# Other queues and moments for layer 0's loads of tables, u and bias, a corner set once, and a priority for evacuations: a two-layer encoder trunk on one core

## The chip, the core and the metric

The kernel runs on one core of a Trainium2 chip. The metric is device time in microseconds of one execution of the whole program. A core has a TensorE (PE) for matmuls and transposes, a VectorE (DVE), a ScalarE (ACT), a GpSimd (POOL), and a SyncE (SP) that only issues DMAs. Each of them works through its own list of instructions in a fixed order, and an instruction that waits holds up everything behind it in that list. DMAs are issued from a list too: here from SP's, and some from POOL's.

## The reference

Two layers work on a sequence of 256 frames of width 2048, in float32. Layer 0 makes one projection of the normalised input, cut into q, k, v for an attention of 16 heads x 64, u for a state-space branch (S5), and two gates:

```
proj = rmsnorm(x) @ w_in                 # q | k | v | u | z_A | z_B
s    = q k^T / sqrt(64) + bias           # own chunk of 64 frames and the chunks before it
o_a  = softmax(s) v * silu(z_A)
x_t  = Abar x_{t-1} + Bbar u_t           # complex, 64 groups of 16 channels, one state of 64 each
y    = gelu(Re(C x_t) + D u_t)
o_b  = y * sigmoid(y @ w_glu + b_glu) * silu(z_B)
x    = x + concat(o_a, o_b) @ w_out
```

With 256 frames every frame sees its own chunk of 64 and all earlier ones, so the score block of frames 0 to 63 against frames 64 to 127 is masked. Layer 1 is an attention with forget gates (16 heads x 128), with its own input projection, gate and output projection. A last RMSNorm follows.

## The kernel before

**Weights.** All weights stream through the core once, in tiles of 128 x 1024 float32 (512 KB), one such tile to a *chunk*. `next_w` (line 148) loads a tile from SP's queue into one of four buffers, and a split makes of it a high half (`wh`, ACT, line 164) and a low half (`wl`, DVE, line 165), three buffers each. The split is given priority over other work (`SPLIT_AHEAD`, 3000). `project` (line 168) runs a projection over 16 or 8 blocks of 128 rows, two blocks to a chunk, with three matmuls for each block and each half of the tokens (lines 175 to 177): twelve matmuls of 128 x 512 in a chunk. A projection has two accumulators in PSUM, out of three; after its last chunk the function `evac` empties them (line 191).

**The task clock.** PE's order is written by hand. `tick()` (line 141) counts chunks. Other work is put into tasks, generators that run at a given chunk and say with `yield n` that they go on n chunks later; `at_chunk(c, task)` files one. What a task issues for PE stands at this place between the chunks. For the other engines and for the DMA queues a planner sets the order, from its own estimate of times and from priorities. `high_priority(offset)` raises the priority of an instruction, and `keep_in_program_order` pins a DMA in its queue at its place in the program's order. The chunks of layer 0: u 0 to 15, the first gate `za` 16 to 23, q 24 to 31, k, v, then za, q, k, v of the second half of the heads at 48 to 79, the gate `zb` 80 to 95, the attention's output projection `oa` from 96.

**S5.** `setup_task` (line 724) computes small tables and loads the first two `bc` (B and C of eight groups, 256 KB). `tables(e, ...)` (line 343), for e from 0 to 7, works a `bc` into larger tables on DVE and ACT (lines 351 to 380), stores `mx` to DRAM (`m_d`, line 381), and after `gap` chunks (12 for the first, 6 for the others) transposes on PE (`pm`), a product `pk`, four stores of `ks` to DRAM (`k_d`, line 402), the next `tables`, and the load of `bc` e + 2 (line 408). There are two buffers of `bc`. After a further wait (`READY`: the first one not before chunk 28) come `pv`, transposes, and copies to the state `X`. `u_in` (line 434) starts at chunk 16. It loads u back from DRAM as `un` (four loads on SP's queue, line 439), spreads it on ACT seven chunks later (`spread`, line 443, behind the newest split in ACT's order), and transposes it two chunks on (`pu`, line 456; the last two of four a chunk after the first two) into `uT`. From chunk 64 `load_T` and `load_mo` (lines 632 and 639) read the stored tables back from POOL's queue.

**Attention of layer 0.** The 16 heads are worked in two halves (`a0`, `a1`), each in four pairs of heads. `pair(hp)` (line 579) loads the bias tile `bt` (128 x 2 x 256, two buffers, each load into a fresh tile, line 584), sets its masked corner of 64 partitions x 64 columns on POOL (line 585), turns q and k two chunks later (`pqk`), makes the scores a chunk after that (`psc`), lets `probs` (line 523) do the softmax on DVE and ACT, and turns the result four chunks later (`turn_probs`, `pp`, line 547). `mix` (line 601) multiplies by v. The list at line 752 says at which chunk each pair and mix starts. `gate_T` (line 494) is the first gate: evacuated by ACT with SiLU (line 500), then turned (`pz`). `load_xa` (line 711) brings the residual input into the buffers that q, k, v and a gate leave.

**Layer 1** (from line 820) runs four groups of four heads, each with projections q, k, v and z of 16 blocks.

Of the kernel before, what the change touches and what calls it, by code (L numbers as in the profile page):

```python
# [9 lines left out]
F32 = mybir.dt.float32  # L10
# [7 lines left out]
P = 128  # L18
L = 256
# [4 lines left out]
NEG = -1.0e30  # L24
# [14 lines left out]
SPLIT_AHEAD = 3000  # L39
# [4 lines left out]
def trunk(ctx: ExitStack, tc: tile.TileContext, a, out: bass.AP):  # L44
    nc = tc.nc
# [73 lines left out]
    def at_chunk(c, task):  # L119

        seq[0] += 1
        queue.append((c, seq[0], task))
        if not busy:
            run_due()
# [16 lines left out]
    def tick():  # L141
        clock[0] += 1
        run_due()
# [4 lines left out]
    def next_w(split=None, dst=None):  # L148
        i = wpos[0]
        wpos[0] += 1  # L150
        raw = wp.tile([P, CK * NT], F32, name=f"wr_{i}", tag="wr", bufs=4)
        if dst:
            wh, wl = dst
        else:
            wh = wp.tile([P, CK * NT], F32R, name=f"wh_{i}", tag="wh", bufs=3)
            wl = wp.tile([P, CK * NT], F32R, name=f"wl_{i}", tag="wl", bufs=3)
        step = NT if split else CK * NT
        for o in range(0, CK * NT, step):
            c = slice(o, o + step)
            nc.sync.dma_start(raw[:, c], a["w"][i][:, c])  # L160
            if split:
                split(o // NT)
            with tc.high_priority(offset=SPLIT_AHEAD):
                last_split[:] = [nc.scalar.activation(wh[:, c], raw[:, c], AF.Copy)]  # L164
                nc.vector.tensor_tensor(wl[:, c], raw[:, c], wh[:, c].bitcast(F32), op=ALU.subtract)  # L165
        return wh, wl

    def project(ah, al, nkb, name, evac, ready=None, by_token=False):

        acc = [ps_acc.tile([P, NT], F32, name=f"acc_{name}_{t}", tag="acc") for t in range(2)]  # L170

        def block(kb, wh, wl, t):
            c = slice(kb % CK * NT, (kb % CK + 1) * NT)
            sh, sl = ah[:, kb, t * P:(t + 1) * P], al[:, kb, t * P:(t + 1) * P]
            nc.tensor.matmul(acc[t], sh, wh[:, c], start=kb == 0, stop=False)  # L175
            nc.tensor.matmul(acc[t], sh, wl[:, c], start=False, stop=False)  # L176
            nc.tensor.matmul(acc[t], sl, wh[:, c], start=False, stop=kb == nkb - 1)  # L177

        if by_token:
            for t in range(2):  # L180
                for kb in range(nkb):
                    block(kb, *ready[kb // CK], t)
            return acc
        for kc in range(nkb // CK):
            wh, wl = ready[kc] if ready else next_w()
            kbs = range(kc * CK, (kc + 1) * CK)
            for kb, t in [(kb, t) for kb in kbs for t in range(2)] if ready else [(kb, t) for t in range(2) for kb in kbs]:
                block(kb, wh, wl, t)
            if kc == nkb // CK - 1:
                for t in range(2):  # L190
                    evac(t, acc[t])
            tick()


# [4 lines left out]
    at = l0.enter_context(tc.tile_pool(name="at", bufs=2))  # L199
# [137 lines left out]

    def load_bc(e):
        bc = s5.tile([P, 8, 4, GC], F32, name=f"bc_{e}", tag="bc", bufs=2)
        tc.keep_in_program_order(nc.sync.dma_start(bc, a["s5bc"][:, e * 8:e * 8 + 8]))  # L340
        return bc

    def tables(e, bc, gap, ready):
# [35 lines left out]
        V.tensor_tensor(tm, pw(pi, fwd), wide(bc[:, :, 3, :], 8), op=ALU.mult)  # L379
        V.tensor_tensor(mx[:, :, 1:9, :], mx[:, :, 1:9, :], tm, op=ALU.add)  # L380
        nc.sync.dma_start(m_d[e], mx[:, :, 1:9, :].rearrange("p s l c -> p s (l c)"))

        yield gap

# [18 lines left out]
        if e == 7:  # L403
            at_chunk(clock[0], s5_tail())
        else:
            at_chunk(clock[0], tables(e + 1, bcs[e + 1], GAPS[e + 1], READY[e + 1]))
            if e < 6:
                bcs.append(load_bc(e + 2))
        yield max(2, ready - clock[0])

        pv = ps_s.tile([P, 2, P], F32, name=f"pv_{e}", tag="s")
# [15 lines left out]
            nc.scalar.copy(X[:, 1:, w, e * 8:e * 8 + 8],  # L427
                           pt[:, w].rearrange("p k (g n) -> p n (k g)", n=NCH))

    GAPS, READY = (12, 6, 6, 6, 6, 6, 6, 6), (28, 0, 0, 0, 0, 0, 0, 0)  # L430
    uT = s5b.tile([P, NGQ, P], F32, name="uT")
    un = X = None

    def u_in():

        nonlocal un, X
        un = res.tile([P, TC, G * GC // 4], F32, name="un", tag="X")
        for g4 in range(4):
            nc.sync.dma_start(un[32 * g4:32 * g4 + 32],
                              u_d[:, g4 * 256:(g4 + 1) * 256].rearrange("(n j) f -> n j f", j=TC))  # L440
        un4s = []

        def spread(b):
            un4 = s5b.tile([P, 4, TC, GC], F32, name=f"un4_{b}", tag="vs", bufs=2)
            with tc.issue_after(last_split[0].ins):
                nc.scalar.copy(un4, un[:, ::-1, b * 64:(b + 1) * 64].rearrange("p j (k c) -> p k j c", c=GC))
            un4s.append(un4)

        yield 7
        spread(0)  # L450
        spread(1)
        yield 2
        for b in range(4):
            pu = ps_s.tile([P, 4, P], F32, name=f"pu_{b}", tag="s")
            for k in range(4):
                nc.tensor.transpose(pu[:, k, :], un4s[b][:, k].rearrange("p j c -> p (j c)"), ident)
            nc.scalar.copy(uT[:, b * 4:b * 4 + 4, :], pu)
            if b < 2:
                spread(b + 2)
            if b == 1:  # L460
                yield 1
        X = res.tile([P, NCH + 1, 2, G], F32, name="X", tag="X")
        nc.gpsimd.memset(X[:, 0], 0.0)
# [50 lines left out]
    def scores(qT, kT, rows, keys):  # L514

        pscs = [ps_s.tile([P, 3, P], F32, name=f"psc_{key}", tag="s") for key in keys]
        for psc, r in zip(pscs, rows):
            nc.tensor.matmul(psc[:, 0, :], qT[r, 0:P], kT[r, 0:P], start=True, stop=True)
        for psc, r in zip(pscs, rows):
            nc.tensor.matmul(psc[:, 1:3, :], qT[r, P:L], kT[r, 0:L], start=True, stop=True)  # L520
        return pscs
# [41 lines left out]
            nc.vector.tensor_tensor(dl[:, kb + k, :], po[:, k], dh[:, kb + k, :].bitcast(F32), op=ALU.subtract)  # L563

    rbx = a["rbx"]

    class Half:

# [10 lines left out]
        def pair(self, hp):  # L579

            hf = self.hf
            h0 = hf * 8 + hp * 2
            bt = at.tile([P, 2, L], F32, name=f"bt_{hf}_{hp}", tag="bt")
            nc.sync.dma_start(bt, bass.AP(rbx.tensor, rbx.offset + h0 * 384, [[1, P], [384, 2], [1, L]]))
            nc.gpsimd.memset(bt[0:64, :, 0:64], NEG)
            yield 2
            pqk = ps_s.tile([P, 2, L], F32, name=f"pqk_{hf}_{hp}", tag="s")
            for w, src in ((0, self.q), (1, self.k)):
                for t in range(2):
                    nc.tensor.transpose(pqk[:, w, t * P:(t + 1) * P], src[:, t, hp * P:(hp + 1) * P], ident)  # L590
            qkT = at.tile([P, 2, L], F32, name=f"qkT_{hf}_{hp}", tag="qkT")
            nc.scalar.copy(qkT, pqk)
            yield 1
            pscs = scores(qkT[:, 0, :], qkT[:, 1, :], [slice(0, 64), slice(64, 128)], [f"a{h0}", f"a{h0 + 1}"])
            lgs = [probs(at, pscs[hh], bt[:, hh, P - 1::-1], bt[:, hh, ::-1], f"a{h0 + hh}", scaled=True)
                   for hh in range(2)]
            yield 4
            for hh in range(2):
                self.work.append(turn_probs(at, lgs[hh], f"a{h0 + hh}", scaled=True))
# [27 lines left out]
    a0, a1 = Half(0), Half(1)  # L627
# [83 lines left out]
    def load_xa(n):  # L711
        t_ = at.tile([P, 2, NT], F32, name=f"xa_{n}", tag=("qk", "qk", "v", "za")[n], bufs=(2, 2, 1, 3)[n])
        nc.sync.dma_start(t_, xin[:, :, n * NT:(n + 1) * NT])
        xa.append(t_)

    def load_xas(*ns):
        for n in ns:
            load_xa(n)
        yield None
# [11 lines left out]
    bcs = []  # L731
# [18 lines left out]
    at_chunk(clock[0], u_in())  # L750

    for c, task in ((39, a0.pair(0)), (43, a0.pair(1)), (49, a0.mixes(0)), (47, a0.pair(2)), (52, a0.mixes(1)),
                    (51, a0.pair(3)), (56, a0.mixes(2)), (60, a0.mixes(3)),
                    (71, a1.pair(0)), (75, a1.pair(1)), (81, a1.mixes(0)), (79, a1.pair(2)), (84, a1.mixes(1)),
                    (83, a1.pair(3)), (88, a1.mixes(2)), (92, a1.mixes(3)), (93, load_xas(0, 1, 2)), (96, load_xas(3))):
        at_chunk(c, task)
    zb = []
    a0.zaT = gate_T(0)
# [26 lines left out]
    for n in range(2):  # L785
# [4 lines left out]
        def evac(t, acc):  # L790
            V.tensor_tensor(ob[:, t, :], acc, bg, op=ALU.add)
            nc.scalar.activation(ob[:, t, :], ob[:, t, :], AF.Sigmoid)
            V.tensor_tensor(ob[:, t, :], ob[:, t, :], zb[n][:, t, :], op=ALU.mult)
# [223 lines left out]
    acc = project(oTh, oTl, 16, "oo3", None, held, by_token=True)  # L1017
# [95 lines left out]
```

## Time and profile before

| | us |
|---|---|
| median of three runs | 968.06 (966.23 to 968.22) |
| the profiled execution, its own time | 967.27 |
| its span, first to last instruction | 965.6 |
| TensorE busy | 933.5 |
| VectorE busy | 579.4 |
| ScalarE busy | 517.0 |
| GpSimd busy | 104.4 |

The profile is one execution. Its page lists busy times and the costliest groups of instructions; other views of the same trace list who waited for whom, the instructions of an engine in order of time, and the busy time of every engine in a stretch. A wait is noted with the instruction that waited, what released it, the total, the number of times and the longest one. In the timelines the columns are start, duration, engine, line, operation, output from inputs, the count of merged instructions, and in brackets the idle time before with what ended it. In the table of stretches the columns are the stretch, its length, the busy time (and instructions) of PE, PE's weight loads, DVE, ACT and POOL, then the granted clock of TensorE as a share of full speed, the busy share of the DMA engines, and GB/s.

### The profile page before, as it was taken

How to read it: one execution, taken by the hardware profiler on the slowest of the kernel's cores; microseconds unless marked ns; L12 is line 12 of the kernel's file. 1: busy time of each engine (PE TensorE's matmuls, PEld its weight loads, DVE VectorE, ACT ScalarE, POOL GpSimd, SP SyncE). 2: the span in 40 equal slices, each digit the busy share in tenths (PEclk: the TensorE clock that was granted, in tenths of full speed). 3: DMA queues.
4: the chain of work that ended last, by engine and by line, in shares of the span. 5: the costliest groups of instructions: out<-in, count | busy, mean ns of one | idle time of the engine just before them, and what ended most of it. 6: DMA issues, size and time to landing. Idle time of an engine off the chain costs nothing.

```text
span 965.6 us, 13241 instructions
## 1 busy us (share of the span) xinstructions
PE 933.5 (97%) x4814; PEld 758.8 (79%) x4814; DVE 579.4 (60%) x1023; ACT 517.0 (54%) x817; POOL 104.4 (11%) x177
## 2 busy tenths in 40 slices
PE   6997999999998999999999999999999999999995
PEld 5885777777776678788888888888888888888884
DVE  7886678755798346665755545454545454545573
ACT  6636556864464666455645644464446444644451
POOL 2000000000652000200001400040004000200210
PEclk9999999999999899999999999999999999999998
DMA  9877566645999468655556555555554556455552
GB/s 326 289 222 230 178 203 203 193 156 185 227 232 305 161 224 247 219 174 182 179 195 226 174 186 174 190 171 186 173 193 148 184 173 194 152 182 171 195 197 88
DMA packets 68546, 190.43 MB, mean 197 GB/s; under 512 B 7936, under 2 KB 22512, under 8 KB 68096
## 3 DMA queue, kind: packets, MB, share of 16 engines
q1 hardware_dynamic: 65056, 181.07, 58.4%
q0 software_dynamic: 3424, 8.51, 3.5%
q8 instruction: 38, 0.62, 0.3%
q14 instruction: 28, 0.23, 0.1%
HBM read 180.09 MB, written 9.45 MB: 196 GB/s over the span
## 4 chain that ended last, share of the span: by engine, by line
PE 85%; DVE 4%; DMA 3%; ACT 3%; issue 3%; SPq 1%; POOL 0%; POOLq 0%; DVEq 0%; ACTq 0%
PE acc_cq L175 3%; PE acc_cv L177 3%; PE acc_ck L175 3%; PE acc_cq L177 3%; PE acc_cv L176 3%; PE acc_cz L177 3%; PE acc_cv L175 3%; PE acc_cq L176 3%; PE acc_cz L175 3%; PE acc_ck L177 3%; PE acc_ck L176 3%; PE acc_cz L176 3%; PE acc_oo L177 3%; PE acc_oo L175 3%; PE acc_oo L176 3%
## 5 line engine op out<-in xcount | busy, mean ns | idle before, releaser
L165 DVE TENSOR_TENSOR wl<-wr,wh 128x1024 fp32r<-128x1024 f32 (+1 forms) x292 | 361.4, 1238 | 288.1 <-ACT wh L164 287.4
L164 ACT ACTIVATE wh<-wr 128x1024 fp32r<-128x1024 f32 (+1 forms) x292 | 310.9, 1066 | 342.4 <-PE acc_cz L177 46.7
L175 PE MATMUL acc_cv<-wh,x1Th 128*128 128x512 f32 x128 | 51.3, 400 | 0.0
L175 PE MATMUL acc_cq<-wh,x1Th 128*128 128x512 f32 x128 | 50.6, 395 | 0.0
L175 PE MATMUL acc_cz<-wh,x1Th 128*128 128x512 f32 x128 | 50.2, 392 | 0.0
L177 PE MATMUL acc_cv<-wh,x1Tl 128*128 128x512 f32 x128 | 50.0, 390 | 0.0
L176 PE MATMUL acc_cv<-wl,x1Th 128*128 128x512 f32 x128 | 49.9, 390 | 0.0
L175 PE MATMUL acc_ck<-wh,x1Th 128*128 128x512 f32 x128 | 49.9, 390 | 0.0
L177 PE MATMUL acc_cq<-wh,x1Tl 128*128 128x512 f32 x128 | 49.9, 390 | 0.0
L176 PE MATMUL acc_cq<-wl,x1Th 128*128 128x512 f32 x128 | 49.8, 389 | 0.0
L177 PE MATMUL acc_cz<-wh,x1Tl 128*128 128x512 f32 x128 | 49.8, 389 | 0.0
L177 PE MATMUL acc_ck<-wh,x1Tl 128*128 128x512 f32 x128 | 49.8, 389 | 0.0
L176 PE MATMUL acc_ck<-wl,x1Th 128*128 128x512 f32 x128 | 49.8, 389 | 0.0
L176 PE MATMUL acc_cz<-wl,x1Th 128*128 128x512 f32 x128 | 49.8, 389 | 0.0
L916 POOL TENSOR_SCALAR cbt<-ckb,cum 128x128 f32<-128x128 f32 x16 | 13.8, 861 | 308.8 <-DVE mx_c L529 261.9
L175 PE MATMUL acc_oo<-wh,oTh 128*128 128x512 f32 x108 | 42.2, 391 | 0.0
L177 PE MATMUL acc_oo<-wh,oTl 128*128 128x512 f32 x108 | 42.0, 389 | 0.0
L176 PE MATMUL acc_oo<-wl,oTh 128*128 128x512 f32 x108 | 42.0, 389 | 0.0
L636 POOL DMA_DIRECT2D T<-k_d x64 | 33.6, 530 | 58.3 <-DMA k_d<-ks 37.0
L175 PE MATMUL acc_u<-wh,xTh 128*128 128x512 f32 x64 | 26.0, 406 | 6.0 <-ACT wh L164 6.0
L175 PE MATMUL acc_q<-wh,xTh 128*128 128x512 f32 x64 | 26.8, 418 | 2.3 <-ACT za L500 2.2
L175 PEld LDWEIGHTS acc_ck<-wh,x1Th 128*128 128x128 f32 x128 | 24.0, 188 | 5.4 <-ACT wh L164 0.4
(407 smaller groups left out, 2080.0 us busy)
## 6 DMA issues: line engine op xcount, KB each, us to landing
wr<-in_w_dram SPq DMA_DIRECT2D x295, 512.0 KB, 3.4
m_d<-mx SPq DMA_DIRECT2D x8, 512.0 KB, 5.7
T<-k_d POOLq DMA_DIRECT2D x64, 64.0 KB, 6.8
mo<-m_d POOLq DMA_DIRECT2D x8, 512.0 KB, 7.2
bt<-in_rbx_dram SPq DMA_DIRECT2D x8, 256.0 KB, 7.6
bc<-in_s5bc_dram SPq DMA_DIRECT2D x8, 256.0 KB, 4.0
xt<-in_x_dram SPq DMA_DIRECT2D x2, 1024.0 KB, 7.2
xa<-in_x_dram SPq DMA_DIRECT2D x4, 512.0 KB, 6.6
```

The lines of the kernel that those rows point to most:

```text
L164: last_split[:] = [nc.scalar.activation(wh[:, c], raw[:, c], AF.Copy)]
L165: nc.vector.tensor_tensor(wl[:, c], raw[:, c], wh[:, c].bitcast(F32), op=ALU.subtract)
L175: nc.tensor.matmul(acc[t], sh, wh[:, c], start=kb == 0, stop=False)
L176: nc.tensor.matmul(acc[t], sh, wl[:, c], start=False, stop=False)
L177: nc.tensor.matmul(acc[t], sl, wh[:, c], start=False, stop=kb == nkb - 1)
L636: nc.gpsimd.dma_start(tt_[j * GC:(j + 1) * GC], k_d[e, :, :, GC * (j + 1):GC * (j + 1) + P])
L916: W.tensor_scalar(bt[:, 0, :], self.ckb[:, hh, 0:P], cum[:, 0, h:h + 1], None, op0=ALU.add)
```

## The change

- `bc` from the third on is loaded from POOL's queue and without a pin; the load is traced right after the store of `mx` in the same `tables`, no longer after the `k_d` stores.
- u is loaded back from POOL's queue. It is spread eight chunks after `u_in` starts instead of seven, and all that follows in `u_in` moves with it; `READY` of the first table goes from 28 to 29.
- The two bias tiles are made once, before both halves, and their corner is set once. Each pair loads its tile in two pieces that leave the corner out. For the first two pairs the loads are pinned.
- The evacuations in `project` get a priority of half the split's.
- `pair(3)` of the first half starts at chunk 55 instead of 51 and its mix at 63 instead of 60; in the second half at 85 instead of 83 and 93 instead of 92. The first three `xa` loads start at 94 instead of 93.

```diff
@@ project
             if kc == nkb // CK - 1:
                 for t in range(2):
-                    evac(t, acc[t])
+                    with tc.high_priority(offset=SPLIT_AHEAD // 2):
+                        evac(t, acc[t])
@@ load_bc
-        tc.keep_in_program_order(nc.sync.dma_start(bc, a["s5bc"][:, e * 8:e * 8 + 8]))
+        if e < 2:
+            tc.keep_in_program_order(nc.sync.dma_start(bc, a["s5bc"][:, e * 8:e * 8 + 8]))
+        else:
+            nc.gpsimd.dma_start(bc, a["s5bc"][:, e * 8:e * 8 + 8])
@@ tables
         nc.sync.dma_start(m_d[e], mx[:, :, 1:9, :].rearrange("p s l c -> p s (l c)"))
+        if e < 6:
+            bcs.append(load_bc(e + 2))
...
             at_chunk(clock[0], tables(e + 1, bcs[e + 1], GAPS[e + 1], READY[e + 1]))
-            if e < 6:
-                bcs.append(load_bc(e + 2))
...
-    GAPS, READY = (12, 6, 6, 6, 6, 6, 6, 6), (28, 0, 0, 0, 0, 0, 0, 0)
+    GAPS, READY = (12, 6, 6, 6, 6, 6, 6, 6), (29, 0, 0, 0, 0, 0, 0, 0)
@@ u_in
-            nc.sync.dma_start(un[32 * g4:32 * g4 + 32],
+            nc.gpsimd.dma_start(un[32 * g4:32 * g4 + 32],
                               u_d[:, g4 * 256:(g4 + 1) * 256].rearrange("(n j) f -> n j f", j=TC))
...
-        yield 7
+        yield 8
         spread(0)
         spread(1)
@@ the bias tiles
     rbx = a["rbx"]
+    bts = [at.tile([P, 2, L], F32, name=f"bt_{i}", tag="bt") for i in range(2)]
+    for bt in bts:
+        nc.gpsimd.memset(bt[0:64, :, 0:64], NEG)
@@ Half.pair
-            bt = at.tile([P, 2, L], F32, name=f"bt_{hf}_{hp}", tag="bt")
-            nc.sync.dma_start(bt, bass.AP(rbx.tensor, rbx.offset + h0 * 384, [[1, P], [384, 2], [1, L]]))
-            nc.gpsimd.memset(bt[0:64, :, 0:64], NEG)
+
+            bt = bts[hp % 2]
+            for p0, c0 in ((0, 64), (64, 0)):
+                ld = nc.sync.dma_start(bt[p0:p0 + 64, :, c0:], bass.AP(
+                    rbx.tensor, rbx.offset + h0 * 384 + p0 + c0, [[1, 64], [384, 2], [1, L - c0]]))
+                if h0 < 4:
+                    tc.keep_in_program_order(ld)
@@ the list of tasks
-                    (51, a0.pair(3)), (56, a0.mixes(2)), (60, a0.mixes(3)),
+                    (55, a0.pair(3)), (56, a0.mixes(2)), (63, a0.mixes(3)),
...
-                    (83, a1.pair(3)), (88, a1.mixes(2)), (92, a1.mixes(3)), (93, load_xas(0, 1, 2)), (96, load_xas(3))):
+                    (85, a1.pair(3)), (88, a1.mixes(2)), (93, a1.mixes(3)), (94, load_xas(0, 1, 2)), (96, load_xas(3))):
```

## The prediction

> **What bounds the kernel now.** I read the page first, then the table of who waited for whom on PE, then the engines' timelines around each wait (where rows of several engines stand in one fence, they are in order of time).
>
> ```profile
> span 965.6 us, 13241 instructions
> PE 933.5 (97%) x4814; PEld 758.8 (79%) x4814; DVE 579.4 (60%) x1023; ACT 517.0 (54%) x817; POOL 104.4 (11%) x177
> ```
>
> TensorE is busy for 97% of the span, and the change takes no matmul away. All that can be won is the time in which PE stands still, or runs slowly after standing still. PE's waits, in full:
>
> ```profile
> PE acc_u L175 <- ACT wh L164: 6.0, 1, 6.0
> PE pp_a L547 <- ACT lg_a L539: 5.8, 1, 5.8
> PE pu L456 <- ACT un L446: 5.1, 1, 5.1
> PE acc_q L175 <- ACT za L500: 2.2, 1, 2.2
> PE acc_u L176 <- DVE wl L165: 1.3, 2, 0.7
> PE acc_za L176 <- DVE wl L165: 0.8, 1, 0.8
> PE acc_za L175 <- ACT wh L164: 0.7, 1, 0.7
> ```
>
> The first row is the start-up before any matmul can run; the fifth is in the first 22 us. The other four places are in layer 0, and I call them **A** (acc_za, 0.7 + 0.8), **B** (pu, 5.1), **C** (acc_q, 2.2) and **D** (pp_a, 5.8): 14.6 us together. No row names an accumulator of layer 1 (acc_c...): nothing is left to win there. Behind B, C and D, the table of busy time by stretch has a second cost:
>
> ```profile
> 75.00:78.00 3.00, 1.57 (x6) 0.77 (x5) 1.95 (x2) 3.00 (x6) 0.00 (x0) 1.00 1.06 369
> ...
> 92.88:96.00 3.12, 3.12 (x11) 2.62 (x12) 1.89 (x2) 2.87 (x5) 0.21 (x1) 0.50 0.47 168
> 208.60:212.10 3.50, 3.50 (x14) 3.03 (x13) 2.01 (x3) 3.50 (x9) 0.00 (x0) 0.51 0.45 138
> 315.90:321.30 5.40, 5.39 (x33) 3.40 (x34) 0.75 (x5) 2.37 (x6) 0.53 (x1) 0.50 0.28 87
> ```
>
> The column after POOL's is the granted clock. It is 0.50 right after each of the three long waits, so half of each stretch is lost: 1.56 + 1.75 + 2.70 = 6.0 us. Across A (75 to 78) it stays at 1.00. **B costs 6.7, C 3.9, D 8.5 and A 1.5: 20.6 us.**
>
> One chunk (twelve matmuls, one tick of the task clock) is the unit of what follows: thirteen matmul starts apart, 2.72 us.
>
> ```profile
> 59.98 0.39 PE L175 MATMUL acc_za<-wh,xTh 128*128 128x512 f32 x1
> ...
> 62.70 0.39 PE L175 MATMUL acc_za<-wh,xTh 128*128 128x512 f32 x1
> ```
>
> **The change, part by part.**
>
> *The u loads (A).* They move to POOL's queue, and spreading and reading them move one chunk later (7 to 8, READY 28 to 29).
>
> ```profile
> 64.08 1.31 SPq L439 DMA_DIRECT2D un<-u_d  x2
> 73.92 1.14 ACT L446 COPY un<-un 128x512 f32<-128x512 f32 x2 [5.52 <-DMA un<-u_d]
> ```
>
> ACT waits 5.52 us for u, and the weight split behind it in its order comes late: that is A. One chunk later is 76.6, after the landing at 73.9, so the wait is gone if POOL's queue delivers within 2.7 us of SP's. SP also loses its own wait for the u writes, behind which weight loads stood. Queued behind POOL's wait are the memset of X and later tables; it has until the first X copy, at chunk 31. POOL pays four issues; the nearest row is 0.53 us for one of T's (quoted below), so 2.1 us, beside an idle POOL. Gain 1.5.
>
> *The tables' loads (B).* bc from the third on go to POOL, unpinned, and are traced right behind the m_d store instead of behind the k_d stores.
>
> ```profile
> 63.17 1.22 DVE L379 TENSOR_TENSOR tm<-pi,bc 128x1024 f32<-128x1024 f32 x1
> 82.13 2.52 SPq L402 DMA_DIRECT2D k_d<-ks  x4
> 84.69 1.00 SPq L340 DMA_DIRECT2D bc<-in_s5bc_dram  x1
> 89.32 0.40 ACT L356 ACTIVATE bc<-bc,nsgn 128x128 f32<-128x128 f32 x1 [6.27 <-DMA bc<-in_s5bc_dram]
> 89.63 0.29 ACT L357 ACTIVATE bc<-bc 128x128 f32<-128x128 f32 x1
> 89.83 1.04 ACT L164 ACTIVATE wh<-wr 128x1024 fp32r<-128x1024 f32 x1
> 90.77 1.05 ACT L507 COPY zaT<-pz 128x512 f32<-128x512 f32 x2
> 91.71 0.59 ACT L457 COPY uT<-pu 128x512 f32<-128x512 f32 x1
> 92.19 0.64 ACT L446 COPY un<-un 128x512 f32<-128x512 f32 x1
> ```
>
> The buffer was free after its last reader (the tm product of the first table), at 64.4, but SP issued the load at 84.7, behind four k_d stores. ACT stood 6.27 us before the tables' scaling, with zaT, uT and un behind it, and PE's pu behind those. Issued at about 65, even twice as long in flight as the 4.6 us here (84.69 to 89.32), bc is there at 75; ACT was free at 83.05 (89.32 less 6.27). If POOL's in-order queue put this load behind the u loads' wait, it would come some 2 us later, which that margin covers. So B goes. What is late next: between the two pairs of pu lies one chunk, 2.72 us, in which ACT has two un copies, two uT copies, a split and perhaps the scaling: 1.28 + 1.18 + 1.04 + 0.69 = 4.2. Bounds of the new wait: 0 (un first: 1.28) to 1.5, or 3.2 with half a window of slow clock as behind C. I take 1.0: the zaT copies now stand a chunk earlier than pu.
>
> [...]
>
> *Evacuations ahead, pair(3) of each half later (C).*
>
> ```profile
> 204.61 0.49 ACT L535 ACTIVATE lg_a<-lg_a,nm_a 128x256 f32<-128x256 f32 x1
> ...
> 205.22 1.28 ACT L500 ACT_TABLE_LOAD   x1
> 206.51 0.69 ACT L500 ACTIVATE za<-acc_za,rs 128x512 f32<-128x512 f32 x1
> ```
>
> The exponentials of pair(3) stand ahead of za's table load and evacuation, which frees the accumulator that acc_q waits for. Two edits each take this away: pair(3) starts at 55 instead of 51, so that its scores come at 58, behind za's last chunk (55), and evacuations have priority over everything but the weight splits. Gain 3.9. Evacuations on DVE (oa, oe) go ahead as well; PE waits for none of them now, so I count them at nothing. What the move carries along: two bt loads (they need the buffer of pair(1), whose scores lie nine chunks back, seven in the second half), four transposes, a copy, four score matmuls, the softmax and its transposes at 62, and mixes(3) at 63 instead of 60; in the second half pair(3) moves by two chunks and mixes(3) by one, to 93. The mixes are needed by the last chunk of oa0, 99, so six chunks cover them. The xa loads go from 93 to 94 on SP, since they reuse the slots of q and k that pair(3) reads; they are first needed at 99 too. All of this costs PE nothing, as no matmul is added. The softmax has four chunks (10.9 us) before its transposes; at D it took 3.5 us from its first DVE instruction at 312.39 (below) to PE's restart at 315.9.
>
> *The corner set once (D).* The eight memsets of bt's corner become two at the start (0.4 us by the row below, before POOL has anything that PE waits for), and each bt load becomes two that leave the corner out: 8 more issues on SP at 0.38 us (the row of the next part), 3.0 us spread over layer 0, beside SP's waits for free weight buffers; without that cover a weight load behind a pair of them would be 0.4 us late, one sixth of a chunk. Gain bounds: nothing to D.
>
> ```profile
> 295.97 0.60 PE L520 MATMUL psc_a<-qkT 64*128 64x256 f32 x4
> 300.28 0.53 POOL L641 DMA_DIRECT2D mo<-m_d  x1 [2.01 <-PE pyi L659]
> 300.80 0.22 POOL L585 MEMSET bt<- 64x128 f32 x1
> 312.39 0.28 DVE L527 CUSTOM_DVE_ANT_0 lg_a<-psc_a,bt 128x128 f32<-128x128 f32 x1
> ```
>
> The scores stood at 296.6, but the memset waited in POOL's order behind T and mo loads until 300.8, and the softmax stands in DVE's order at 312.4, behind splits that wait for PE. The load itself waits only for the softmax two pairs earlier, as before. Without the memset the operands are complete at 296.6. PE wants the result at 310.1 (315.9 less 5.8), so D goes, with its 2.7 us of slow clock. Gain 8.5.
>
> *The first bt loads pinned.* They wait for nothing and were issued at the very start, among the weights and x; the later one:
>
> ```profile
> 9.93 0.38 SPq L584 DMA_DIRECT2D bt<-in_rbx_dram  x1
> ```
>
> 2 x 256 KB at the 369 GB/s of full DMA engines (75 to 78) are 1.4 us, while PE's two start-up waits (acc_u on DVE) are 1.3 us together. Bounds 0 and 1.3; I take 0.6, about the middle, as nothing in the rows says which of the two waits the loads made longer.
>
> **Sum.** The profiled execution took 967.3 us (1.7 around its span), 0.8 under the median of 968.1. 967.3 - 20.6 - 0.6 + 1.0, and 1.4 for two small waits of A's size that a new order on ACT and DVE may leave, is 948.5; against the median, 949.3. I predict **949**.
>
> **Rivals.**
>
> 1. *The transfers themselves are the limit*, and u and bc land no earlier from POOL. For it: the DMA share is 1.06 at A (the row of 75 to 78). Against it: B's late issue. A and B come back: 949 + 8.2 = 957. [...] Chance 0.06.
>
> 2. *POOL issues slowly beside a busy DVE.* Then the u loads land behind 80, where the spreading now stands, and ACT waits for them with splits behind it, as at B: 949 + 6.7 = 956. Against it stands the page's row of T, issued while DVE ran most of the time:
>
> ```profile
> L636 POOL DMA_DIRECT2D T<-k_d x64 | 33.6, 530 | 58.3 <-DMA k_d<-ks 37.0
> ```
>
> [...] Chance 0.04.
>
> 3. *C or D stays, or one of that size appears* (a softmax behind an evacuation). 949 + 3.9 to 949 + 8.5: 953 to 958. For it: the planner writes these orders anew. Chance 0.12.
>
> 4. *It doesn't do what it says:* the planner's order yields other waits of the same sum, 966 to 970. Chance 0.06.
>
> 5. *Slower: evacuations too early on ACT in layer 1.* There are 16 projections there, and PE idles in none. If the planner puts an evacuation ahead of splits, ACT waits for the accumulation to end. The page has a split's two halves:
>
> ```profile
> L165 DVE TENSOR_TENSOR wl<-wr,wh 128x1024 fp32r<-128x1024 f32 (+1 forms) x292 | 361.4, 1238 | 288.1 <-ACT wh L164 287.4
> L164 ACT ACTIVATE wh<-wr 128x1024 fp32r<-128x1024 f32 (+1 forms) x292 | 310.9, 1066 | 342.4 <-PE acc_cz L177 46.7
> ```
>
> With three buffers (line 155) a split may begin two chunks (5.4 us) before PE needs it and takes 1.1 + 1.2: 3.1 us of slack. An evacuation two chunks early costs 5.4 - 3.1 = 2.3 us each, 37 in all: 986. It decides against the change from 1.3 us beyond the slack on each (20.6 / 16). Against it: the splits keep the greater priority (3000 against 1500). Chance 0.13.
>
> **Chances and range.** The forecast has 0.59 and its own range is 946 (nothing left behind, 1.3 at the start) to 954 (3.2 at pu, A back). With rivals 1 to 3 that is 0.81, so the range is 945 (the lower end in the profiled execution's terms) to 961 (rival 3's 958 with 3.2 at pu). Faster by over 0.2% (about what a measurement here can tell from no change): 0.59 + 0.06 + 0.04 + 0.12 = 0.81; same 0.06; slower 0.13.
>
> **What would show it.** Right: PE's table of waits without pp_a, acc_q and acc_za and with under 2 us at pu; granted clock 1.00 from 12 us to the tail; bc issued on POOL near 65; L527 of the third pair of the second half within 3 us of its scores. Wrong: ACT waiting for u or bc; a new row of over 2 us in PE's table; PE idle in layer 1.

## The result, and the profile after

The median went from 967.14 us (965.52 to 968.22) to **955.86** us (954.47 to 957.07): ratio 0.9883, 95% interval 0.9864 to 0.9902. The sign was forecast and the time lies in the range of 945 to 961, but outside the 946 to 954 that the forecast gave itself: 949 was named, and of 19 us that were to go, 11 went. The profiled execution of the new kernel took 957.07 us, the slowest of its four, so some of the small waits below are at the upper end of what they cost.

From the page of the new kernel, the span and the engines:

```profile
span 955.3 us, 13250 instructions
PE 931.4 (97%) x4814; PEld 757.0 (79%) x4814; DVE 579.8 (61%) x1023; ACT 517.2 (54%) x818; POOL 109.7 (11%) x181
```

The span is 10.3 us shorter: 2.1 us of it is busy time of PE, which ran slowly for less time (mean granted clock 0.993, before 0.990); 8.2 us is idle time. Who waited for whom on PE, in full:

```profile
PE acc_u L175 <- ACT wh L164: 6.1, 1, 6.1
PE acc_q L175 <- ACT za L504: 1.9, 1, 1.9
PE pu L460 <- ACT un L450: 0.9, 2, 0.6
PE pp_a L551 <- ACT qkT L603: 0.9, 1, 0.9
PE acc_u L176 <- DVE wl L165: 0.9, 2, 0.5
PE psc_a L522 <- ACT min L396: 0.9, 1, 0.9
PE acc_glu L175 <- DVE xa L785: 0.9, 1, 0.9
PE acc_za L176 <- DVE wl L165: 0.7, 1, 0.7
PE acc_q L176 <- DVE wl L165: 0.2, 1, 0.2
```

The rows of 5.8 (pp_a behind lg_a) and 5.1 (pu) are gone. In their place stand an acc_q row that looks like the old C but lies at the *first* gate, at 81.6, and several rows of 0.9 that stood nowhere before. Two of the stretches behind them, in the table of busy time by stretch, ran at a lower clock:

```profile
81.60:85.00 3.40, 3.40 (x11) 2.71 (x12) 3.40 (x4) 1.91 (x3) 0.55 (x1) 0.54 0.23 54
162.17:166.60 4.43, 4.43 (x15) 3.15 (x16) 4.43 (x9) 1.83 (x6) 0.00 (x0) 0.62 0.75 238
```

3.40 x 0.46 + 4.43 x 0.38 = 3.2 us are lost there. The waits after the start-up are 0.9 at pu, 0.7 + 0.2 at acc_za and the second acc_q row, and 1.9 + 0.9 + 0.9 + 0.9; with the 3.2 that makes 9.6 us, where the prediction left 2.4 (1.0 at pu and 1.4 for two small waits). This difference of 7.2 is most of the 8.6 by which the profiled execution missed its own sum (957.1 to 948.5).

Where do these waits come from? Two of ACT's waits for DMAs, in the first 400 us of the same trace:

```profile
ACT bc L360 <- DMA bc<-in_s5bc_dram: 11.6, 5, 5.5
...
ACT un L450 <- DMA un<-u_d: 1.5, 1, 1.5
```

ACT still waits for both loads that the change was to bring early. Around the pair at 160 to 162 us, the timelines of POOL, ACT and PE together, in order of time:

```profile
145.72 0.55 POOL L344 DMA_DIRECT2D bc<-in_s5bc_dram  x1 [18.75 <-ACT wh L164]
145.86 0.28 ACT L423 COPY vs<-pv 128x128 f32<-128x128 f32 x1
151.68 0.40 ACT L360 ACTIVATE bc<-bc,nsgn 128x128 f32<-128x128 f32 x1 [5.54 <-DMA bc<-in_s5bc_dram]
...
160.12 0.57 ACT L603 COPY qkT<-pqk 128x512 f32<-128x512 f32 x1
160.74 0.55 PE L551 MATMUL pp_a<-ident,lg_a 128*128 128x128 f32 x3 [0.89 <-ACT qkT L603]
161.54 1.05 ACT L396 COPY min<-pm 128x512 f32<-128x512 f32 x2
162.17 0.85 PE L522 MATMUL psc_a<-qkT 64*128 64x128 f32 x3 [0.88 <-ACT min L396]
```

POOL issues the load at 145.7, as soon as its buffer is free (the last reader, tm, ends at 145.2), and ACT stands from 146.1 to 151.7 before the scaling of *that* load. Nobody needs it yet: it is the table after the next. The softmax's exponentials, a copy of q and k and the copy of `min` stand behind it in ACT's order, and PE runs into both copies late. The same order at the first gate:

```profile
74.29 1.14 ACT L450 COPY un<-un 128x512 f32<-128x512 f32 x2 [1.48 <-DMA un<-u_d]
75.44 0.40 ACT L360 ACTIVATE bc<-bc,nsgn 128x128 f32<-128x128 f32 x1
...
79.57 1.28 ACT L504 ACT_TABLE_LOAD   x1
80.86 0.69 ACT L504 ACTIVATE za<-acc_za,rs 128x512 f32<-128x512 f32 x1
81.60 0.79 PE L175 MATMUL acc_q<-wh,xTh 128*128 128x512 f32 x1 [1.87 <-ACT za L504]
```

The wait for u (1.48) and a scaling (0.7 with its second half) lie ahead of the first gate's evacuation. And where B was, a scaling stands again:

```profile
89.90 0.40 ACT L360 ACTIVATE bc<-bc,nsgn 128x128 f32<-128x128 f32 x1 [3.31 <-DMA bc<-in_s5bc_dram]
```

This is not the scaling that stood there before (that one is done at 75.4) but the one for the next load of bc, issued at 84.0. The copies of uT and un for pu follow it in ACT's order. The hypothesis for the experiments: *because bc is now loaded as soon as a buffer is free, the planner also puts its scaling there, one table ahead, and ACT waits in its order for a load that nobody needs yet.*

### The profile page after: what moved, and what is told of

It reads as the page before. It is cut to its first block, busy times and chain, and to the rows that moved or that the text cites. A ratio compares the mean times of both kernels' runs of the same rounds, so it can differ in the third digit from the quotient of the medians.

```text
span 955.3 us, 13250 instructions
## 1 busy us (share of the span) xinstructions
PE 931.4 (97%) x4814; PEld 757.0 (79%) x4814; DVE 579.8 (61%) x1023; ACT 517.2 (54%) x818; POOL 109.7 (11%) x181
## 4 chain that ended last, share of the span: by engine, by line
PE 80%; issue 2%; ACT 1%; DMA 1%; DVE 0%; POOLq 0%; POOL 0%; DVEq 0%; ACTq 0%
PE acc_cq L175 3%; PE acc_cv L177 3%; PE acc_ck L175 3%; PE acc_cv L176 3%; PE acc_cq L177 3%; PE acc_cq L176 3%; PE acc_cv L175 3%; PE acc_ck L176 3%; PE acc_cz L175 3%; PE acc_cz L176 3%; PE acc_cz L177 3%; PE acc_ck L177 3%; PE acc_oo L175 3%; PE acc_oo L176 3%; PE acc_oo L177 3%; PE acc_zb L175 2%
```

## The experiments

Each ratio is to the kernel before, measured beside it. The expectations number their theories; what each says stands in them.

**No priority for the evacuations.**

```diff
-                    with tc.high_priority(offset=SPLIT_AHEAD // 2):
-                        evac(t, acc[t])
+                    evac(t, acc[t])
```

> The changed kernel without the priority of evacuations; everything else stays. Theory 1 (the waits that are left come from loads: ACT waits for the next table's bc and for u, and what stands behind it in its order is late): the priority moves nothing that PE waits for, since pair(3) already starts behind the gate's end. 956 within 2 us, PE's waits at acc_q, pu, pp_a and psc_a as they are. Theory 2 (the left-over waits come from the new order that the priority makes on ACT): acc_q, pp_a and psc_a go, with their slow clock, 949 to 952. Theory 3 (the priority is what removed the old wait at the second gate): acc_q waits 2.2 us more near chunk 56, 959 to 960.

955.5 us, 0.9884 (0.9861 to 0.9907): the priority changes nothing as long as pair(3) starts later. PE waits nowhere in layer 1, with it or without it.

**The bias tiles as before:** a fresh tile for each pair, one load, the memset on POOL.

```diff
-            bt = bts[hp % 2]
-            for p0, c0 in ((0, 64), (64, 0)):
...
+            bt = at.tile([P, 2, L], F32, name=f"bt_{hf}_{hp}", tag="bt")
+            nc.sync.dma_start(bt, bass.AP(rbx.tensor, rbx.offset + h0 * 384, [[1, P], [384, 2], [1, L]]))
+            nc.gpsimd.memset(bt[0:64, :, 0:64], NEG)
```

> The changed kernel with the bias tiles as before: one fresh tile and one load for each pair, the corner set by POOL each time, no pins. Theory 1 (POOL's memset behind the T and mo loads was what made the softmax late at D): the wait of 5.8 us at pp_a comes back in the second half with 2.7 us of slow clock, and two early loads at the start cost up to 1.3: 964 to 966. Rival (the later start of pair(3) and the new order already cure D): 956 to 957, no wait of over 1 us at pp_a after chunk 80.

965.99 us, 1.0001 (0.9983 to 1.0018): the whole gain is gone. In the table of PE's waits, D is back to the tenth:

```profile
PE pp_a L551 <- ACT lg_a L543: 5.8, 1, 5.8
```

D is not all of it. POOL issues u's loads at 62.9 here instead of 58.1, ACT waits 7.3 us for u, and PE waits 2.0 us at 79 to 80: the bias part moves u as well.

**The tables' loads as before:** SP's queue, pinned, behind the `k_d` stores.

```diff
-        if e < 2:
-            tc.keep_in_program_order(nc.sync.dma_start(bc, a["s5bc"][:, e * 8:e * 8 + 8]))
-        else:
-            nc.gpsimd.dma_start(bc, a["s5bc"][:, e * 8:e * 8 + 8])
+        tc.keep_in_program_order(nc.sync.dma_start(bc, a["s5bc"][:, e * 8:e * 8 + 8]))
...
             at_chunk(clock[0], tables(e + 1, bcs[e + 1], GAPS[e + 1], READY[e + 1]))
+            if e < 6:
+                bcs.append(load_bc(e + 2))
```

> The changed kernel with the bc loads as before: SP's queue, pinned, behind the k_d stores. Theory 1 (the issue's place sets the wait): ACT again waits over 5 us for bc before pu, PE waits 5 us at pu instead of 0.9 and runs slowly after it: 956 + 4.2 + 1.6 = 962, less up to 3.5 if the wait at pp_a and psc_a, which stands behind a bc load of the changed kernel, goes: 958 to 962. Rival (the transfers are the limit, the place of the issue changes nothing): 956 within 1 us.

950.48 us, 0.9837 (0.9810 to 0.9863): *faster* than the whole change, which no theory had foreseen. The load is issued late again, behind the four stores, and ACT stands before its scaling, as SP's and ACT's timelines show in order of time:

```profile
81.76 0.58 SPq L341 DMA_DIRECT2D bc<-in_s5bc_dram  x1
85.44 0.40 ACT L357 ACTIVATE bc<-bc,nsgn 128x128 f32<-128x128 f32 x1 [3.87 <-DMA bc<-in_s5bc_dram]
```

ACT's waits for bc even add up to 13.4 us, more than the 11.6 of the changed kernel. But PE's wait at pu is 1.0 at most, and acc_q, pp_a and psc_a are gone from its table:

```profile
PE pu L457 <- ACT un L447: 1.3, 2, 1.0
```

So B goes without the early load of bc, and something else cures it. The early load, with what comes along with it, costs 5 us instead. And a sum of ACT's waits is not a price: what counts is what stands behind each of them in ACT's order when PE wants it.

**u as before:** SP's queue, spread seven chunks after, READY 28.

```diff
-            nc.gpsimd.dma_start(un[32 * g4:32 * g4 + 32],
+            nc.sync.dma_start(un[32 * g4:32 * g4 + 32],
...
-        yield 8
+        yield 7
```

> The changed kernel with u loaded from SP's queue and spread at 7 chunks, READY 28. Theory 1 (A as predicted): ACT's wait for u of 5.5 us and PE's 1.5 us at acc_za come back, 957 to 958. Rival (u from POOL lands as late as it did from SP, 12.5 us in flight instead of 5.5, so the part gains nothing, and the wait of 1.9 us at acc_q with its slow clock belongs to it): 952 to 956.

954.68 us, 0.9877 (0.9856 to 0.9898). A does not come back: ACT has no wait for u here. What comes back is a part of B, in spite of the early bc:

```profile
PE pu L460 <- ACT un L450: 2.7, 1, 2.7
```

The bc that B hung on is there early (its scaling stands at 74.75), but ACT waits 3.15 us before the scaling of the *next* bc, at 88.79, with uT and un for pu behind it. So this run shows that the early load alone, with its scalings free to move, leaves a wait at pu; it doesn't show what an early load with the scalings held would do without the shift.

**pair(3) and its mix at their old chunks**, with the priority kept.

```diff
-                    (55, a0.pair(3)), (56, a0.mixes(2)), (63, a0.mixes(3)),
+                    (51, a0.pair(3)), (56, a0.mixes(2)), (60, a0.mixes(3)),
...
-                    (85, a1.pair(3)), (88, a1.mixes(2)), (93, a1.mixes(3)), (94, load_xas(0, 1, 2)), (96, load_xas(3))):
+                    (83, a1.pair(3)), (88, a1.mixes(2)), (92, a1.mixes(3)), (93, load_xas(0, 1, 2)), (96, load_xas(3))):
```

> The changed kernel with pair(3), mixes(3) and the xa loads at the chunks of before. Theory 1 (the softmax of the fourth pair standing ahead of the second gate's evacuation was C): the priority alone may hold C off; if it does, 956 within 1.5; if not, 2.2 us at acc_q near chunk 56 with 1.7 of slow clock come back, 959 to 960. Rival (the moves cost time, by crowding the chunks 57 to 63): 953 to 954.

954.01 us (the median of three executions; a fourth took 5317 us and is left out), 0.9872 (0.9845 to 0.9899). C stays away from the second gate with the priority alone, as it did with the moves alone. Whether the moves themselves cost a microsecond, as the rival had it, can't be told within these intervals.

**The bias part alone**, on the kernel before: `bts`, its two memsets, and the loads in two pieces.

```diff
+    bts = [at.tile([P, 2, L], F32, name=f"bt_{i}", tag="bt") for i in range(2)]
+    for bt in bts:
+        nc.gpsimd.memset(bt[0:64, :, 0:64], NEG)
```

> The kernel before with only the bias part: two tiles made once, the corner set once, loads in two pieces, the first pairs pinned. Theory 1: D and its slow clock go, and up to 0.6 at the start: 8.5 to 9.1 us under the kernel before. Rival (D needs the later pair(3) too): 0 to 3 us under it.

955.38 us, 0.9882 (0.9853 to 0.9912): this part alone gives as much as the whole change, and more than the 9.1 us that its expectation allowed. Of PE's waits those of over 1.2 us after the start, and then SP's timeline around u's loads:

```profile
PE pu L456 <- ACT un L446: 3.8, 1, 3.8
PE acc_q L175 <- ACT za L500: 1.9, 1, 1.9
```

```profile
58.88 2.25 SPq L439 DMA_DIRECT2D un<-u_d  x2
61.23 0.54 SPq L160 DMA_DIRECT2D wr<-in_w_dram  x1
61.88 1.19 SPq L439 DMA_DIRECT2D un<-u_d  x2
```

D is gone. And SP issues u's loads at 58.9 where it had issued them at 64.1, so ACT has no wait for u left and A's place at 76 is empty: one more gain of an edit that does not touch u. The planner made SP's order anew; why it came out so is not settled. B and C remain, at 3.8 and 1.9, but in this profile C has no slow clock behind it (the granted clock stays at 1.00; 1.7 us were lost in the kernel before; the row is shown in the last section).

**u one chunk later alone**, on the kernel before, from SP's queue.

```diff
-        yield 7
+        yield 8
```

> The kernel before with u spread and turned one chunk later (8 for 7, READY 29), u and bc still from SP's queue. Theory 4 (formed from the run with the old tables' loads: B goes because pu stands a chunk later, not because bc comes early): PE's wait at pu falls from 5.1 to about 1.3 and its slow clock goes, and A's 1.5: 6 to 7 us under the kernel before. Rival (the prediction's reason: B hangs on bc's issue behind k_d): pu still waits over 4 us, 1 to 2 us under the kernel before.

961.92 us, 0.9958 (0.9938 to 0.9978). PE's table has no row for pu at all, with bc loaded exactly as before: **the shift by one chunk cures B.** It gave 4 us and not 6.7 because acc_q now waits at both gates, 2.1 of it at the first with slow matmuls behind it (those of acc_q that start from 82.3 to 88.0 take 0.59 to 0.79 us each, from 88.4 on 0.39 to 0.40), where the spreading of u stands ahead of za's evacuation:

```profile
PE pp_a L547 <- ACT lg_a L539: 5.8, 1, 5.8
PE acc_q L175 <- ACT za L500: 4.4, 2, 2.3
```

**The scalings held**, on the changed kernel: they may stand in ACT's order only behind the newest split, so not one table ahead.

```diff
+        with tc.issue_after(last_split[0].ins):
-        nc.scalar.activation(bc[:, :, 2, :], bc[:, :, 2, :], AF.Copy, scale=nsgn)
-        nc.scalar.activation(bc[:, :, 3, :], bc[:, :, 3, :], AF.Copy, scale=-1.0)
+            nc.scalar.activation(bc[:, :, 2, :], bc[:, :, 2, :], AF.Copy, scale=nsgn)
+            nc.scalar.activation(bc[:, :, 3, :], bc[:, :, 3, :], AF.Copy, scale=-1.0)
```

> The changed kernel with the two ACT scalings of each bc held behind the newest weight split in ACT's order, as the spreading of u is; bc still comes from POOL. Theory 1 (with the earlier bc the planner moves each table's scalings a whole table ahead, so that ACT waits in order for a load that nobody needs yet; 5.5 us of it stand before the softmax at pp_a and psc_a, and it made the za evacuation late): ACT's waits for bc (11.6 us) nearly vanish, PE's waits at pp_a, psc_a and acc_q with their slow clock go: 949 to 951. Rival (bc through POOL costs by its transfers, not by the scalings' place): 955 to 957.

950.22 us, 0.9826 (0.9806 to 0.9846): 5.6 us below the changed kernel. The view of the tile bc gives the scalings' times, first and last start, in the changed kernel and then with the hold:

```profile
L360 ACT ACTIVATE bc<-bc,nsgn x8: 398/402/403, 21.8 to 174.6; 128x128 f32<-128x128 f32 x8
```

```profile
L361 ACT ACTIVATE bc<-bc,nsgn x8: 382/384/398, 47.2 to 192.1; 128x128 f32<-128x128 f32 x8
```

The last one moves from 174.6 to 192.1, about one table (six chunks) later, ACT has no wait for bc left, and the rows pp_a, psc_a and pu are gone from PE's table. The hypothesis holds.

**Held, and bc from SP behind `k_d`** (this edit and that of the third experiment together).

> The changed kernel with bc from SP behind the k_d stores, as before, and the two scalings held behind the newest split. Theory 1 (the place of the scalings in ACT's order makes the waits, not the queue of bc): no ACT wait for bc near pu, 949 to 951, the same as with bc from POOL and the scalings held (950.2). Rival (bc from POOL is worth something once the scalings are held): 952 to 954, with ACT waiting for bc behind k_d.

949.16 us, 0.9819 (0.9803 to 0.9835), against 950.22 and 0.9826: with the scalings at their place, queue and moment of bc's load make no difference that can be told. ACT does wait 3.1 us for bc here, at 85.8, where theory 1 had none; PE waits 0.9 at pu.

**Held, and u's loads from SP**, still spread at chunk eight.

```diff
-            nc.gpsimd.dma_start(un[32 * g4:32 * g4 + 32],
+            nc.sync.dma_start(un[32 * g4:32 * g4 + 32],
```

> The changed kernel with the scalings held and u loaded from SP's queue, still spread at 8. Theory 5 (u lands no earlier from POOL, since its transfers share the full DMA engines: 12.5 us in flight there, 5.5 from SP): ACT's wait for u of 1.5 us stays or goes, the time is that of the held scalings within 1.5 us: 949 to 952. Rival (SP's own wait for the u writes, with weight loads behind it, is what POOL's queue saves): ACT waits longer for weights after 60 us, PE waits over 1 us more around 76: 952 to 955.

948.53 us, 0.9810 (0.9796 to 0.9825). How long u's four loads took, in the view of the tile un: first in the changed kernel, from POOL, then here, from SP:

```profile
DMA to landing us min/median/max: 10.7/12.5/14.2
```

```profile
DMA to landing us min/median/max: 4.0/5.5/6.9
```

From SP they are issued at 57.7 to 61.6 (from POOL at 58.1 to 59.9), take half as long, and ACT does not wait for them. The acc_q wait of 0.9 that the held kernel still had at the first gate is gone.

**Held, and zb times y on DVE.** In the held kernel PE waited 0.8 at acc_glu for the residual additions on DVE. The timelines of POOL and DVE in the held kernel show why DVE is late:

```profile
368.37 5.75 POOL L721 TENSOR_TENSOR zb<-zb,y 128x1024 f32<-128x1024 f32 x2 [36.33 <-DMA y<-y_d]
369.35 2.50 DVE L165 TENSOR_TENSOR wl<-wr,wh 128x1024 fp32r<-128x1024 f32 x1 [1.50 <-ACT wh L164]
372.08 3.12 DVE L165 TENSOR_TENSOR wl<-wr,wh 128x1024 fp32r<-128x1024 f32 x1 [0.22 <-ACT wh L164]
```

Two splits beside POOL's products take 2.50 and 3.12 us, where one takes 1.24 on average (the group in the page of before). So the product goes to DVE:

```diff
-            nc.gpsimd.tensor_tensor(zb[n], zb[n], y, op=ALU.mult)
+            nc.vector.tensor_tensor(zb[n], zb[n], y, op=ALU.mult)
```

> The changed kernel with the scalings held, and the product of the second gate with y (two multiplications, 128 x 1024) on VectorE instead of GpSimd. Theory 6 (VectorE's low half, which reads two operands from SBUF, is held up by GpSimd's multiplication, which does too: 2.5 and 3.1 us instead of 1.23, and PE's 0.8 us at acc_glu is behind it): every low half near 370 us takes 1.23 us, the wait at acc_glu goes: 0.5 to 0.9 us less than with the scalings held alone, 949.4. Rival (the long low halves wait for something else): they stay long, and VectorE's added 2.3 us make acc_glu later: 950 to 952.

948.39 us, 0.9812 (0.9796 to 0.9828). DVE's timeline at this place:

```profile
366.31 1.22 DVE L721 TENSOR_TENSOR zb<-zb,y 128x1024 f32<-128x1024 f32 x1 [1.78 <-DMA y<-y_d]
367.46 1.22 DVE L165 TENSOR_TENSOR wl<-wr,wh 128x1024 fp32r<-128x1024 f32 x1
```

The product takes 1.22 us instead of 2.9, the splits are back to their length, and the acc_glu row is gone. The acc_q wait of 0.9 is absent here too, though this edit doesn't touch it (u landed in time in this run), and the acc_glu wait was absent in the run before. So these two runs don't price each of the two waits of 0.8 to 0.9 by itself, and their ratios, 0.9810 and 0.9812, have intervals that overlap with that of the held kernel (0.9806 to 0.9846): it is shown that the waits go, not what that is worth. The next run has both edits.

**All three together:** scalings held, u from SP, the product on DVE.

> The changed kernel with the scalings held, u from SP's queue and the gate's product on VectorE, all three. Theory: the three remove different waits of PE (pp_a and psc_a; acc_q behind u; acc_glu), of which the runs alone have left under 1.5 us each: PE's waits after the start-up fall to under 1.5 us in all, 947 to 949. Rival (what is left is in the start-up and the tail, and the three give nothing more together): the same as u from SP alone, 948.5 within 0.7.

**947.02** us (946.70 to 947.58) against 965.97, ratio 0.9799 (0.9782 to 0.9815): the lowest of all, clear of the changed kernel (0.9864 to 0.9902), though not of the three runs just above. PE's waits in full:

```profile
PE acc_u L175 <- ACT wh L164: 6.2, 1, 6.2
PE acc_za L176 <- DVE wl L165: 0.7, 1, 0.7
PE acc_u L176 <- DVE wl L165: 0.4, 1, 0.4
```

Nothing after the first gate's start is left (the acc_za row is at its first split, at 57.9; the changed kernel has it at 57.1), and the granted clock is 1.00 in the stretches from the start to 900 us.

## Why the prediction was right, and where it was not

**D, right.** The memset in POOL's order was what the softmax waited for; taken away, PE stops nowhere near, and the softmax stands 1.0 us behind its scores (within 3 had been asked). The timeline of the changed kernel:

```profile
292.29 0.60 PE L524 MATMUL psc_a<-qkT 64*128 64x256 f32 x4
...
293.90 0.28 DVE L531 CUSTOM_DVE_ANT_0 lg_a<-psc_a,bt 128x128 f32<-128x128 f32 x1
```

8.5 us had been named; putting the old bias tiles back costs some 10, and the part alone gains 10.7 (966.04 to 955.38). What goes beyond 8.5 was not forecast: the part also moves u's loads, and in its profile the slow clock behind C is missing.

**C, right, and either edit is enough.** Without the priority, and with the old chunks, the second gate has no wait. But the prediction looked only at the gate where C was. An almost equal wait came at the first one, 1.9 us with 1.6 us lost to slow clock behind it. It is not C that moved there, but A.

**B, the gain right, the reason wrong.** The step that failed is "So B goes", worked out from the issue of bc at 84.7 and the 6.27 us that ACT stood before the scaling. The load did what was asked: it was issued at 68.3 (near 65 had been said) and scaled at 75.4. But ACT's wait at this place stayed, because the scaling of the next bc came there: 3.31 us at 89.9, where 6.27 at 89.3 had been. With bc back at its late place, pu waits 1.0 at most; with the shift of u alone, not at all; with bc early and u unshifted, 2.7. One chunk later for pu is enough for ACT to be through its list. That the 6.7 came out all the same is luck. The chain had been read rightly. What was overlooked was that the term under A, "spreading and reading them move one chunk later", moved B's own deadline as well. The wait that was forecast to replace it, 1.0, is 0.9.

**A, moved and not gained.** "So the wait is gone" is the step that failed here. The waits at 76 went, but what ACT has to do between u's spreading and the first gate's evacuation stayed, and u came no earlier. The evacuation in the kernel before:

```profile
80.84 0.69 ACT L500 ACTIVATE za<-acc_za,rs 128x512 f32<-128x512 f32 x1
```

In the changed kernel it starts at 80.86 (the row is shown above). PE no longer stops at 76; it comes to acc_q sooner, waits there 1.87, starts its seventh matmul of acc_q at 81.60 (81.58 before), and loses 1.6 to slow clock besides. The wait for u at ACT is 1.48, which the prediction had named as a sign against it. With the bias part alone, where SP issues u's loads 5 us earlier, the evacuation starts at 79.31, PE does not wait at this gate, and A is gained.

POOL issues u's loads 6 us earlier than SP did before, but they land at 74.3 instead of 73.9. The DMA engines are full from 60 to 74 (a share of 1.01), and SP's weight loads run beside u's. SP's timeline, first in the changed kernel, then with u on SP (scalings held), where u's loads are issued at 57.7 and 61.0:

```profile
57.08 10.11 SPq L160 DMA_DIRECT2D wr<-in_w_dram  x5
```

```profile
60.35 0.54 SPq L160 DMA_DIRECT2D wr<-in_w_dram  x1
...
62.24 5.97 SPq L160 DMA_DIRECT2D wr<-in_w_dram  x4
```

From SP, all but one of these weight loads stand behind u in the same queue, and u takes 5.5 us at a share of 0.90 (58 to 72; 1.06 from 64 on). In the author's reading an order among the loads fits this better than full engines alone; no run separates it from a slower POOL queue. Rival 1, that the transfers are the limit, was right about u, which landed no earlier from POOL, and wrong about bc, which did. For u the other queue gained nothing, and there was a loss in flight: the medians are 9.4 to 12.5 us from POOL (in five profiles) and 5.3 to 6.1 from SP (in six).

**"1.4 for two small waits of A's size", mis-sized.** This term held all that a new order on ACT and DVE could leave, and 1.4 was taken with no instruction named. In its place stand 1.9 at acc_q, 0.9 at each of pp_a, psc_a and acc_glu, 0.9 at acc_za and acc_q's second row, and 3.2 of slow clock: 8.7 us. The 5.6 that come back when the scalings are held come from an operation which the prediction had counted as removed from the way. It followed bc's *load* through POOL's queue and never asked where its *reader* would go: it moved with the load, one table ahead, and the load issued at 145.7 took until 151.7. (That the planner put it there by an estimate that had the load land sooner is likely from how it works, but no run shows it by itself.)

**Start-up.** 0.6 had been taken; the two acc_u rows went from 7.3 to 7.0 in sum. The profiles of the other runs with the new bias tiles lie between 6.6 and 7.9, so no gain is shown. (One reading in passing: the two rows that give a chunk's length are twelve matmul starts apart, not thirteen; 2.72 us is right.)

**The other rivals.** Rival 2: an issue of u from POOL took 0.59 us beside a DVE that was busy for all of it (2.00 us of the 2.00 from 58 to 60), 0.06 more than T's 0.53. Rival 3 (953 to 958) is nearest to what happened, in the form "one of that size appears": an evacuation at the first gate is late behind u and a scaling, and copies at 160 to 162 are late behind another scaling. Rival 5, the slower one: PE doesn't wait in layer 1, where ACT's evacuations wait at most 0.3 us each for their accumulation; taking the priority away changes nothing.

**The signs.** Of those named for being right, the wait at pu (0.9) and the softmax at D held. PE's table still has rows of pp_a, acc_q and acc_za, at other places, and the clock fell to 0.54 and 0.62 in two stretches. Of those named for being wrong, one came: ACT waits for u and for bc.

## What to carry to other kernels

When a load is moved earlier and a planner or a list scheduler sets the order, follow the first instruction that *reads* it: it moves too, and on an engine that works in order it can wait for the load ahead of work that is due (here ACT for 5.54 us, with the softmax behind it). Price a wait on such an engine by what stands behind it when the bound engine wants it, not by its length: 13.4 us of waits for bc cost little (950.5, and 949.2 with the scalings held), and 11.6 at other places cost over 5. Where several edits are made at once, run each alone: here one of them gave the whole gain, one was worth less than nothing, and one cured a wait for which another had been meant. And when a wait is taken away, look where the bound engine arrives next: at A the next event on ACT came no earlier, so the wait only moved.

## What the hardware showed besides

**GpSimd in VectorE's way.** A product of two SBUF tiles on POOL (two of them, 2.9 us on average) stretched the splits beside it from 1.2 us to 2.5 and 3.1, and they are back at 1.22 with the product on DVE. In the rows of the held kernel the second product ends at 374.12 and the second split at 375.20, 1.1 us later, while a split alone takes 1.22: as if it had only begun when POOL was done. The kernel before shows the same at its own product (392.68 and 393.77). That is a reading of these ends; what holds the split up is not shown.

**A wait's length doesn't settle the clock.** 1.87 us at acc_q in the changed kernel was followed by 3.4 us at a granted clock of 0.54 (the row of 81.60 above). A wait of 1.9 us, of the bias part alone, was followed by none; the clock stayed at 1.00:

```profile
205.96:209.36 3.40, 3.40 (x19) 2.92 (x20) 1.57 (x2) 3.40 (x8) 0.00 (x0) 1.00 0.24 59
```

And two waits of 0.9 with 1.4 us from one to the next, at 160 to 162 in the changed kernel, were followed by a slow stretch as well (4.43 us at 0.62). What decides besides the length of a wait is not shown by these runs.
